# Output projection of a hybrid decoder step: from plain tiles to Strassen's scheme on halves, with tokens stationary

## The chip, the cores and the metric

The kernel runs on one NeuronCore of a Trainium2 chip. Five engines work side by side, each through its own instructions in order: TensorE (PE, with its weight loads shown apart as PEld), VectorE (DVE), ScalarE (ACT), GpSimd (POOL) and SyncE (SP), which here issues nearly all DMAs. The metric is the device time of one execution in microseconds; less is better. Matmul operands lie in SBUF (128 partitions), sums in PSUM (eight banks of 128 x 512 float32).

## The reference, cut to what matters

One layer of a hybrid decoder on 1024 prompt tokens with 16 meta tokens ahead of them, and on 32 sample tokens (8 sequences of 4) with 1024 cached positions each. The input projection feeds a stick-breaking attention group and a gated linear attention (GLA) group. Their gated outputs are joined and go through one output projection, a norm and a residual:

```python
mixed = jnp.concatenate([o_sb * jax.nn.silu(sg), o_gla * jax.nn.silu(gg)], axis=-1)
y = mixed @ w_out                      # 2048 features -> 2048 columns
x = x + rms_norm(y, norm_post_g)       # for 1024 prompt tokens and 32 sample tokens
```

All arithmetic is float32. A product of two float32 matrices is made on TensorE of three products: each operand is split into a high part (a cast to fp32r) and a low part (the remainder), and high x high, high x low and low x high are summed in PSUM.

## The kernel before, in words

The kernel is a row of stages, each one a scope of tile pools: transposing and normalising x, the attention heads with the input projection of their columns, GLA, the sample tokens' paged values, and the output projection. A small scheduler in the program, the `Weaver` (`W`), lays side work among the matmuls: a generator is put in with `W.spawn(gen, delay)`, and each `W.beat()` (one after each group of matmuls) runs the generators that are due; a generator's `yield n` asks for its next turn n beats later. Around this, the tile framework sets waits and the order of each engine's instructions: tiles of one tag share a fixed number of buffers, and a new tile waits until the tile whose buffer it takes has had its last reader. Work inside `urgent()` is ordered ahead of other work that is ready.

Weights of all projections come through `weight_chunk` (L174 to L183): a DMA of two blocks of 128 x 128 (128 KB, L177), a cast of the high part on ACT (L181), a subtraction for the low part on DVE (L182). The tags `wr`, `wh` and `wl` have three buffers each.

The gated mixture lies in DRAM as 16 tensors `md[k]`, features on partitions and 1056 token columns. The output projection (from L1158) takes the tokens in two halves `hf`: 512 prompt tokens and the 32 sample tokens together (544), then 512 prompt tokens. For each half `load_mix` (L1166) brings the sixteen `md` tiles into the SBUF slots `s0` to `s15` and splits them. Then for each of 16 blocks `c` of 128 output columns, eight weight chunks pass by, and `project` (L1264) does for each chunk and each column group 2 x 3 matmuls with the weights stationary and the tokens moving: two groups of 272 tokens in the first half, one of 512 in the second, and 256 for the last two blocks, whose split weights are kept in slots (`wk`) so that the last tokens can be finished in two parts. The result has output columns on partitions. `y_tok` (L1201) turns it with PE transposes through `yt` (L1274, L1207; samples L1216), squares it for the norm (L1210) and multiplies by the norm's gain into `y` (L1211). `finish0` (L1220) adds the residual for the first half in pieces of 256 columns (L1233, L1234, store L1236) while the second half is projected, and `finish1` (L1249) does it at the end for two tiles of 128 tokens at a time (L1253, `rstd_` L159 to L165, L1260, store L1262).

In the attention stage `z_feed` (L341 on) computes the sample tokens' scores from the cached keys `kp` on DVE (L376), one page per two beats, with loads on SP (L334).

## Time and profile before

| | |
|---|---|
| median of 3 runs | 2216.09 us (2214.83 to 2216.6) |
| profiled execution | 2214.65 us, its span 2212.9 us |
| busy share of the span | PE 97%, PEld 90%, DVE 72%, ACT 48%, POOL 4% |
| moved by DMA | 267.53 MB, 121 GB/s on average |
| first and last matmul of the output projection | start at 1801.4 and 2199.99 us |

The span runs from the first to the last instruction. A matmul's duration in a row contains its way through the array, and matmuls overlap; what a matmul costs on PE is the distance between the starts of two of them. A row of groups gives line, engine, operation, the output and inputs by the program's names, shapes, count, busy time, the mean of one in ns, and what ended the idle time before them. A row of the timeline begins with the start and the duration in microseconds. In a row of windows stand the stretch, the busy time of each engine with its instructions in brackets, the granted TensorE clock, the share of the sixteen DMA engines and GB/s.

### The profile page before, as it was taken

The page shows a single profiled execution, that of the slowest core. Times are in us where ns is not written, and L with a number is a line of the kernel's source. Part 1 is how long each engine was busy: PE and PEld are TensorE (multiplying, and loading weights), DVE is VectorE, ACT ScalarE, POOL GpSimd, SP SyncE. Part 2 cuts the span into 40 slices and gives each one's busy share as a digit, 9 for nine tenths or more (in the row PEclk, how much of TensorE's full clock was granted, in tenths as well). Part 3 has the DMA queues.
Part 4 walks back from the last instruction along what each step waited for, and adds up shares of the span by engine and source line. Part 5 has one row for each costly group of instructions (what it writes and reads, how often), then busy time and mean ns, then how long its engine had stood idle before and what let it go on. Part 6 is the DMA issues. An engine that isn't in the chain of part 4 may idle for free. (4 is left out here: it accounts for less than half of the span.)

```text
span 2212.9 us, 46718 instructions
## 1 busy us (share of the span) xinstructions
PE 2150.0 (97%) x13712; PEld 1988.2 (90%) x13712; DVE 1593.0 (72%) x6809; ACT 1059.4 (48%) x2900; POOL 87.2 (4%) x299
## 2 busy tenths in 40 slices
PE   6999999999999999999999999999999999999997
PEld 5999999999999989889998989987777899998786
DVE  7367777777777787887777888689999765335434
ACT  7355556555565555325243352444433355444443
POOL 0000010000100000200000000000000000000000
PEclk9999999999999999999999999999999999999999
DMA  6223343433433434324334343356666654225733
GB/s 190 63 75 104 83 106 94 102 105 80 108 97 95 105 80 126 108 74 106 102 89 114 83 116 82 90 161 194 201 193 193 191 179 142 86 84 170 238 96 134
DMA packets 411299, 267.53 MB, mean 121 GB/s; under 512 B 49378, under 2 KB 393890, under 8 KB 409890
## 3 DMA queue, kind: packets, MB, share of 16 engines
q1 hardware_dynamic: 408850, 264.27, 42.5%
q8 instruction: 108, 1.77, 0.3%
q14 instruction: 149, 1.22, 0.2%
q10 hardware_dynamic: 2192, 0.27, 0.1%
HBM read 223.47 MB, written 40.95 MB: 119 GB/s over the span
## 5 line engine op out<-in xcount | busy, mean ns | idle before, releaser
L376 DVE SCALAR_TENSOR_TENSOR jk<-kp,qb 128x128 f32<-128x128 f32 x2048 | 486.9, 287 | 40.9 <-DMA kp<-in_cache_k_dram 38.0
L286 PE MATMUL acc_g<-hT,wh_g 128*128 128x368 f32 (+2 forms) x768 | 258.0, 336 | 0.2
L287 PE MATMUL acc_g<-hT,wh_g 128*128 128x368 f32 (+2 forms) x768 | 247.6, 322 | 0.0
L288 PE MATMUL acc_g<-hT,wl_g 128*128 128x368 f32 (+2 forms) x768 | 246.9, 322 | 0.0
L1269 PE MATMUL oacc<-mx,wh_o 128*128 128x272 f32 (+1 forms) x736 | 238.8, 325 | 6.3 <-ACT wh_o L181 4.4
L1271 PE MATMUL oacc<-mx,wl_o 128*128 128x272 f32 (+1 forms) x736 | 235.5, 320 | 0.0
L1270 PE MATMUL oacc<-mx,wh_o 128*128 128x272 f32 (+1 forms) x736 | 234.8, 319 | 0.2 <-DVE mx L1186 0.2
L182 DVE TENSOR_TENSOR wl_o<-wr_o,wh_o 128x256 fp32r<-128x256 f32 x240 | 101.4, 425 | 152.4 <-ACT wh_o L181 146.3
L286 PEld LDWEIGHTS acc_g<-hT,wh_g 128*128 128x128 f32 x768 | 144.2, 188 | 33.6 <-issue 21.8
L376 DVE DVE_READ_ACCUMULATOR jk<-kp,qb 128x1 f32 x2048 | 166.0, 81 | 0.0
L181 ACT CAST wh_o<-wr_o 128x256 fp32r<-128x256 f32 x240 | 96.7, 405 | 138.7 <-PE oacc L1270 100.9
L1269 PEld LDWEIGHTS oacc<-mx,wh_o 128*128 128x128 f32 x736 | 139.1, 189 | 17.8 <-ACT wh_o L181 6.9
L1271 PEld LDWEIGHTS oacc<-mx,wl_o 128*128 128x128 f32 x736 | 138.6, 188 | 10.2 <-DVE wl_o L182 1.3
L1270 PEld LDWEIGHTS oacc<-mx,wh_o 128*128 128x128 f32 x736 | 138.9, 189 | 8.6 <-DVE mx L1186 0.5
L287 PEld LDWEIGHTS acc_g<-hT,wh_g 128*128 128x128 f32 x768 | 144.4, 188 | 1.1 <-issue 0.4
L288 PEld LDWEIGHTS acc_g<-hT,wl_g 128*128 128x128 f32 x768 | 144.3, 188 | 0.4 <-issue 0.4
L286 PE MATMUL acc_gv<-hT,wh_gv 128*128 128x384 f32 (+1 forms) x384 | 128.7, 335 | 0.0
L286 PE MATMUL acc_k<-hT,wh_k 128*128 128x378 f32 (+1 forms) x384 | 127.8, 333 | 0.0
L181 ACT CAST wh_g<-wr_g 128x256 fp32r<-128x256 f32 x128 | 51.7, 404 | 155.4 <-PE acc_g L287 140.1
L286 PE MATMUL acc_q<-hT,wh_q 128*128 128x368 f32 (+2 forms) x384 | 125.6, 327 | 0.0
L288 PE MATMUL acc_gv<-hT,wl_gv 128*128 128x384 f32 (+1 forms) x384 | 125.4, 327 | 0.0
L287 PE MATMUL acc_k<-hT,wh_k 128*128 128x378 f32 (+1 forms) x384 | 125.2, 326 | 0.0
(399 smaller groups left out, 5904.6 us busy)
## 6 DMA issues: line engine op xcount, KB each, us to landing
kp<-in_cache_k_dram SPq DMA_DIRECT2D x512, 64.0 KB
vr<-in_cache_v_dram SPq DMA_DIRECT2D x64, 512.0 KB
wr_o<-in_w_out_dram SPq DMA_DIRECT2D x256, 128.0 KB
qb<-qsd SPq DMA_DIRECT2D x64, 256.0 KB
wr_g<-in_w_in_dram SPq DMA_DIRECT2D x128, 128.0 KB
wr_v<-in_w_in_dram SPq DMA_DIRECT2D x64, 128.0 KB
wr_k<-in_w_in_dram SPq DMA_DIRECT2D x64, 128.0 KB
wr_q<-in_w_in_dram SPq DMA_DIRECT2D x64, 128.0 KB
```

The costliest lines, as they stand in the source:

```text
L181: act.copy(wh, raw[:])
L182: vec.tensor_tensor(wl, raw[:], wh.bitcast(F32), ALU.subtract)
L286: mm(acc[c][:, :n], wh[:, k2, :], hh[k][:, lo:hi], start=(k == 0), stop=False)
L287: mm(acc[c][:, :n], wh[:, k2, :], hl[k][:, lo:hi], start=False, stop=False)
L288: W.mark = mm(acc[c][:, :n], wl[:, k2, :], hh[k][:, lo:hi], start=False, stop=(k == NK - 1)).ins
L376: ins = vec.scalar_tensor_tensor(jk[:], kp[:], 1.0, qbs[h, b][:, t, :], ALU.mult, ALU.mult, accum_out=zt[:, t, NPG - 1 - i:NPG - i])
L1269: mm(o_, wh[:, k2, :], mh[:, lo:hi], start=(k == 0), stop=False)
L1270: mm(o_, wh[:, k2, :], ml[:, lo:hi], start=False, stop=False)
L1271: mm(o_, wl[:, k2, :], mh[:, lo:hi], start=False, stop=(k == NK - 1))
```

## The change

The output projection is written anew. Features, output columns and, within each half of 512 prompt tokens, tokens are cut in two: `A` (256 x 1024 blocks) times `W` (1024 x 1024 blocks). Seven products of half blocks take the place of eight (Strassen's scheme in Winograd's form). For each token half `hf` and each half `q` of the 1024 columns of a block, `run` goes through the seven products `p` in a written order; each product is four steps `i` of two feature tiles. The split token forms are stationary (128 tokens), 512 weight columns move, so the sums have tokens on partitions and no transposes are left. One step is 2 tiles x 2 token groups x 3 = 12 matmuls of 512 columns; in the products 1, 2, 7 and 3 of the first half 4 more for the 32 sample tokens, whose high and low parts stand side by side as one stationary operand of 64 columns. That is 4 x 7 x 4 x 12 = 1344 and 128 matmuls.

- `weight_forms` makes the four combined weight blocks during attention and GLA and writes them to DRAM (`td`): sixteen rounds with four loads of 256 KB, four subtractions of 128 x 512 on DVE and four stores of 256 KB, from beat 150 on, 40 beats apart.
- `weights` loads 512 KB per step, from `w_out` or `td`, into one of four `raw` buffers, and splits it into one of two places of a `ring` (in the slots `s2`, `s3`).
- `form_a11`, `form_a` and `form_s` load `md` into the same `raw` buffers, form the token combinations on DVE and split them into the slots. For the second half they run while the first half's last products are made, and at the start of its own.
- `into_y` adds each product's sums into tiles `y` of 128 x 512 (18 buffers), and where a tile is complete it squares it and multiplies it by the gain.
- `finish0` and `finish1` do norm and residual per 128 x 512 tile. At the very end the last product is done token group by token group, with its weights kept in slots, so that one tile of 128 tokens is left.

```diff
+    td = [dram.tile([P, 8, 1024], F32, name=f"td{j}") for j in range(4)]
...
+    def weight_forms():
+        for k in range(8):
+            for q in range(2):
+                t = dk.tile([P, 4, 512], F32, tag="tf", bufs=1, name=f"tf{k}_{q}")
+                for i, (r, c) in enumerate(((0, 0), (0, 1), (1, 1), (1, 0))):
+                    r0, c0 = 1024 * r + k * P, 1024 * c + q * 512
+                    nc.sync.dma_start(t[:, i, :], w_out[0, r0:r0 + P, c0:c0 + 512])
+                yield 12
+                vec.tensor_tensor(t[:, 0, :], t[:, 1, :], t[:, 0, :], ALU.subtract)
+                vec.tensor_tensor(t[:, 1, :], t[:, 1, :], t[:, 2, :], ALU.subtract)
+                yield 4
...
+                for j, i in enumerate((0, 2, 1, 3)):
+                    nc.sync.dma_start(td[j][:, k, q * 512:(q + 1) * 512], t[:, i, :])
+                yield 24
...
+        W.spawn(weight_forms(), 150, lasting=True)
...
+        def raw_tile(nm):
+            return op.tile([P, 1024], F32, tag="raw", bufs=4, name=nm)
+        def split(dst, src):
+            act.copy(dst[:, 0], src)
+            vec.tensor_tensor(dst[:, 1], src, dst[:, 0].bitcast(F32), ALU.subtract)
...
+        def form_a(hf):
+            for i in range(4):
+                keep(4 + i, pair(hf, 8 + 2 * i, f"rb{hf}_{i}"), 2 * i, f"fb{hf}_{i}", 2, 4)
+                yield 1
+        def form_s(hf):
+            for i in range(4):
+                u = pair(hf, 2 * i, f"ru{hf}_{i}")
+                v = pair(hf, 8 + 2 * i, f"rv{hf}_{i}")
...
+                vec.tensor_tensor(v1, u1, v1, ALU.add)
+                vec.tensor_tensor(u1, u1, u0, ALU.subtract)
+                vec.tensor_tensor(u0, v1, u0, ALU.subtract)
+                vec.tensor_tensor(v0, v0, u0, ALU.subtract)
+                yield 1
+                keep(8 + i, u, 2 * i, f"fu{hf}_{i}", 6, 7)
+                keep(12 + i, v, 2 * i, f"fv{hf}_{i}", 3, 5)
+                yield 1
...
+        def weights(p, q, i, nm, dst=None):
+            with urgent():
+                r = raw_tile(f"rw{nm}")[:].rearrange("p (k n) -> p k n", k=2)
...
+                nc.sync.dma_start(r, src)
+                if dst is None:
+                    j = next(turn) % 2
+                    dst = [t[:, j * 1024:(j + 1) * 1024].rearrange("p (k n) -> p k n", k=2) for t in ring]
+                act.copy(dst[0], r)
+                vec.tensor_tensor(dst[1], r, dst[0].bitcast(F32), ALU.subtract)
...
+        def product(bank, t, p, i, w, first, last):
+            for j in range(2):
+                a = forms[p, 2 * i + j]
+                ah, al = (a[:, s_, t * P:(t + 1) * P] for s_ in range(2))
+                mm(bank[t][:], ah, w[0][:, j], start=first and j == 0, stop=False, skip_group_check=True)
+                mm(bank[t][:], ah, w[1][:, j], start=False, stop=False, skip_group_check=True)
+                mm(bank[t][:], al, w[0][:, j], start=False, stop=last and j == 1, skip_group_check=True)
...
+        YB = 18
+        YO, XO, TO = (1, 4, 2, 6, 5, 7, 3), (6, 5, 7, 3, 1, 4, 2), (1, 6, 5, 2, 3, 7, 4)
+        run(0, 0, YO, dict(A="acc", B="B", D="D", E="D"), y[0], ssq[0], {})
+        run(0, 1, XO, dict(A="acc", B="B", D="D", E="B"), y[0], ssq[0],
+            {(3, 1): lambda: W.spawn(form_s(1), 2), (1, 1): lambda: W.spawn(form_a11(1), 1), (2, 1): lambda: W.spawn(form_a(1))})
+        W.spawn(finish0(y[0], ssq[0]))
+        W.spawn(finish_samples())
+        run(1, 0, YO, dict(A="acc", B="B", D="D", E="D"), y[1], ssq[1], {})
+        W.flush()
+        run(1, 1, TO, dict(A="acc", B="B", D="D", E="acc"), y[1], ssq[1],
+            {(1, 1): lambda: put_xr(0, 0), (3, 1): lambda: W.spawn(finish1(y[1], ssq[1], xr, (0, 1)), 1),
+             (7, 1): lambda: put_xr(2, 8), (4, 0): lambda: W.spawn(finish1(y[1], ssq[1], xr, (2,))),
+             (4, 1): lambda: W.spawn(finish1(y[1], ssq[1], xr, (3,)))})
-        def load_mix(hf):
-        def y_tok(hf, c, yt, y, ssq, tiles=(0, 1, 2, 3)):
-        def project(hf, kk, wh, wl, acc, yt, lo, hi):
...
-    nc = bacc.Bacc("TRN2", target_bir_lowering=False, num_devices=1)
+    nc = bacc.Bacc("TRN2", target_bir_lowering=False, num_devices=1, dynamic_dma_scratch_size=1024)
```

More of the change, by code (lines that the diff above doesn't have):

```diff
@@ new lines, in pair, with keep @@
+        def pair(hf, k, nm):
+            r = raw_tile(nm)[:].rearrange("p (k n) -> p k n", k=2)
+            for j in range(2):
+                nc.sync.dma_start(r[:, j, :], md[k + j][:, hf * 512:(hf + 1) * 512])
+            return r
+        def keep(i, r, k, nm, p0, p1):
+            f = slot(i, nm).rearrange("p (s k n) -> p s k n", s=2, k=2)
+            split(f, r)
+            for j in range(2):
+                forms[p0, k + j] = f[:, :, j, 0:256]
+                forms[p1, k + j] = f[:, :, j, 256:512]
@@ L1196, in hybrid_step @@
+        for _ in form_a11(0):
+            pass
+        ring += [slot(2 + i, f"ring{i}") for i in range(2)]
+        samples = sample_forms()
+        next(samples)
+        W.spawn(samples, 4)
+        W.spawn(form_a(0))
+        W.spawn(form_s(0), 4)
         gpost = op.tile([P, D], F32, tag="gpost", bufs=1, name="gpost")
         nc.sync.dma_start(gpost[:], norm_post_g[0].partition_broadcast(P))
-        ysm = op.tile([P, 4, P], F32, tag="ysm", bufs=1, name="ysm")
-        sssm = op.tile([P, 4], F32, tag="sssm", bufs=1, name="sssm")
@@ L1264, in project @@
-        def project(hf, kk, wh, wl, acc, yt, lo, hi):
-            o_ = acc[:, :hi - lo]
-            for k2 in range(2):
-                k = 2 * kk + k2
-                mh, ml = mix[hf, k]
-                mm(o_, wh[:, k2, :], mh[:, lo:hi], start=(k == 0), stop=False)
-                mm(o_, wh[:, k2, :], ml[:, lo:hi], start=False, stop=False)
-                mm(o_, wl[:, k2, :], mh[:, lo:hi], start=False, stop=(k == NK - 1))
-            if kk == NK // 2 - 1:
-                with urgent():
-                    act.copy(yt[:, lo:hi], o_)
-            W.beat()
```

297 lines of the change are left out of this document (172 added, 125 removed).

## The prediction

> **What bounds the kernel now.** I read the page's busy shares first, then the windows by stage.
>
> ```profile
> span 2212.9 us, 46718 instructions
> PE 2150.0 (97%) x13712; PEld 1988.2 (90%) x13712; DVE 1593.0 (72%) x6809; ACT 1059.4 (48%) x2900; POOL 87.2 (4%) x299
> ```
>
> ```profile
> 600.00:800.00 200.00, 198.35 (x1203) 184.50 (x1202) 154.73 (x806) 113.98 (x289) 17.71 (x58) 1.00 0.36 95
> 1900.00:2000.00 100.00, 100.00 (x805) 99.98 (x805) 38.52 (x103) 45.27 (x159) 0.00 (x0) 1.00 0.29 84
> 2000.00:2100.00 100.00, 97.05 (x472) 79.97 (x471) 50.75 (x143) 41.87 (x148) 0.00 (x0) 1.00 0.70 218
> 2030.00:2040.00 10.00, 10.00 (x47) 8.26 (x47) 4.65 (x13) 3.78 (x14) 0.00 (x0) 1.00 0.95 320
> 2200.30:2212.90 12.60, 0.44 (x2) 0.20 (x2) 6.63 (x14) 1.51 (x7) 0.00 (x0) 0.63 0.48 191
> ```
>
> PE is the bound in all stages; DVE, about half busy in the projection (1900 to 2100), has room there and less in attention (77% in 600 to 800). At 2030 the DMA engines are nearly full at 320 GB/s, or 337 at full share. After 2200.3 PE has no work left: that is the tail. So time falls only if PE's own work in the projection falls, or its waits or the tail. What PE pays per matmul is the distance of starts, in the timeline:
>
> ```profile
> 1925.10 0.29 PE L1269 MATMUL oacc<-mx,wh_o 128*128 128x272 f32 x1
> 1931.48 0.29 PE L1269 MATMUL oacc<-mx,wh_o 128*128 128x272 f32 x1
> 2149.79 0.39 PE L1269 MATMUL oacc<-mx,wh_o 128*128 128x512 f32 x1
> 2153.19 0.39 PE L1269 MATMUL oacc<-mx,wh_o 128*128 128x512 f32 x1
> 2153.65 0.39 PE L1271 MATMUL oacc<-mx,wl_o 128*128 128x512 f32 x1
> 2153.88 0.60 PE L1207 MATMUL yp<-ident,yt 128*128 128x128 f32 x4
> 2154.23 0.48 PE L1269 MATMUL oacc<-mx,wh_o 128*128 128x512 f32 x1
> ```
>
> Between the first two rows lie 51 matmuls of 272 columns: 6.38 / 51 = 0.1251 us each. Between the next two, 15 of 512: 3.40 / 15 = 0.2267. Four transposes cost 2154.23 - 2153.65 - 0.2267 = 0.35, or 0.088 each. A 256-column one, on the line through both matmul prices, is 0.1183 (an estimate).
>
> **PE's work, before and after.** Before: 1536 x 0.1251 = 192.2, 672 x 0.2267 = 152.3, 192 x 0.1183 = 22.7 and 144 transposes x 0.088 = 12.7, together 379.9 us. The stage runs from the first row below to the last, plus about 0.12 for the last matmul: 398.7. So it holds 18.8 us of waits.
>
> ```profile
> 1801.40 0.29 PE L1269 MATMUL oacc<-mx,wh_o 128*128 128x272 f32 x1
> 2199.99 0.28 PE L1271 MATMUL oacc<-mx,wk 128*128 128x256 f32 x1
> ```
>
> After: (1344 + 128) x 0.2267 = 333.7 us, 46.2 less. Of the eighth saved in the prompt's products, the 128 sample matmuls, which pay 512 columns each, take back 29.0. The Trainium skill (TensorE: Matmul & The Clock Gate, Back-to-back issue gap) gives a gap of N/2.4 + 2.5 ns, 215.8 ns for 512 and 115.8 for 272. By it PE's work would go from 356.6 to 317.7, 38.9 less, and the sum below would come out 7 us later; the trace has 226.7 ns, and I keep the rows.
>
> **The new waits.** The weights of a step are cast on ACT, then subtracted on DVE, now 1024 columns at a time into a ring of two places. The rows for such a chain:
>
> ```profile
> 2150.70 0.39 PE L1270 MATMUL oacc<-mx,wh_o 128*128 128x512 f32 x1
> 2151.12 0.41 ACT L181 CAST wh_o<-wr_o 128x256 fp32r<-128x256 f32 x1 [0.95 <-PE oacc L1270]
> 2151.57 0.42 DVE L182 TENSOR_TENSOR wl_o<-wr_o,wh_o 128x256 fp32r<-128x256 f32 x1 [0.93 <-ACT wh_o L181]
> ```
>
> ```profile
> L181 ACT CAST wh_o<-wr_o 128x256 fp32r<-128x256 f32 x240 | 96.7, 405 | 138.7 <-PE oacc L1270 100.9 <-DMA wr_o<-in_w_out_dram 32.0 <-PE oacc L1271 3.0
> L1185 ACT CAST mx<-mraw 128x544 fp32r<-128x544 f32 x16 | 9.9, 643 | 6.7 <-DMA mraw<-md 6.3 <-PE acc_g L288 0.4
> L1034 DVE TENSOR_TENSOR vvr<-vr 128x1024 f32<-128x1024 f32 x13 | 15.9, 1222 | 4.9 <-DMA vr<-in_cache_v_dram 4.0 <-PE dO L1043 0.9
> L1274 ACT COPY yt<-oacc 128x512 f32<-128x512 f32 x14 | 8.1, 582 | 3.7 <-PE oacc L1271 3.6
> L1234 DVE SCALAR_TENSOR_TENSOR y<-y,r_y,xr 128x256 f32<-128x256 f32 x32 | 14.3, 480 | 3.2 <-DMA xr<-in_x_prompt_dram 3.1
> L1260 DVE SCALAR_TENSOR_TENSOR y<-y,r_y,xr 128x512 f32<-128x512 f32 x8 | 5.5, 748 | 0.1
> ```
>
> ```profile
> L462 DVE TENSOR_TENSOR lo_s<-X,hi_s 127x512 fp32r<-127x512 f32 x43 | 29.6, 688 | 1.8 <-ACT hi_s L461 1.7
> ```
>
> The cast starts 0.42 after the start of the matmul that frees its buffer (0.19 after the array is free), the subtraction 0.04 after the cast's end. A cast of 1024 columns, on the line through 405 (256) and 643 ns (544), is 1.04 us; the subtraction 1.22. So a place freed at time 0 holds both parts at 0.19 + 1.04 + 0.04 + 1.22 + 0.06 = 2.55 us. PE meanwhile does one step, 12 x 0.2267 = 2.72, and needs the low part one matmul later, at 2.95. The chain has 0.40 us to spare, 1.3 in steps with samples (16 matmuls). DVE's whole work of the stage is 112 x 1.22 for weights, 28 x 1.22 + 32 x 0.69 for forms, 80 x 0.69 into y, 32 x 0.48 and 16 x 0.75 for the ends and some 8 for samples: 283 us, less than the stage. It is no bound, but an operation begun at the wrong moment makes a step late. The terms, each with its ends:
>
> (a) While forms are loaded they take every second raw buffer, so weights have two of the four. The cycle is then: subtraction done, DMA of 512 KB, cast, subtraction. The nearest 512 KB load:
>
> ```profile
> 1589.90 1.24 SPq L334 DMA_DIRECT2D vr<-in_cache_v_dram  x1
> 1594.57 1.23 DVE L1034 TENSOR_TENSOR vvr<-vr 128x1024 f32<-128x1024 f32 x1 [0.41 <-DMA vr<-in_cache_v_dram]
> ```
>
> 4.67 us, in a stretch with the DMA engines about two thirds busy. Then 4.67 + 1.04 + 0.04 + 1.22 + 0.1 = 7.07 for two steps, 3.53 each, against 2.72 or 3.63 with samples. Most form loads lie beside sample products; some 12 steps (product 4 twice, product 1 of the second half) do not: 12 x 0.81 = 10 us. Ends 0 and 18.
>
> (b) `finish0` and `form_a` of the second half lie on the first 16 steps of `run(1,0)`: 8.4 MB of weights, 8.4 of x and y, 2.1 of md, 18.9 MB in 43.5 us of PE. At 337 GB/s that is 56 us, 12.5 too many, of which the loads in hand cover some 4 (three steps, 8.2, less one load of 4.67); at 320, 59 us. I take 10, ends 0 and 15. That loads come late there already shows in the chain of waits, for loads a quarter as large:
>
> ```profile
> 2079.63 5.69 DMA wr_o<-in_w_out_dram
> ```
>
> The Trainium skill (DMA: Bandwidth & Descriptors, Specifications) puts the HBM limit per core at about 358 GB/s; by it these steps need 52.8 us and the term is 5 instead of 10. No row here goes over 337.
>
> (c) After the first product of `run(1,0)`, six new y tiles are due at 10.9 us and two of the 18 are free; the other four come with stores of `finish0`, whose norm starts some 5 us in. ACT waits there with the weight casts behind it: 3 us, ends 0 and 6. (d) The x tiles of the second half, 2 MB at once ahead of weights in SP's queue, 6.2 us of DMA at 337 GB/s against 8 us of weights in hand: 2, ends 0 and 4. (e) Evacuations: at the ends of 28 products adds on DVE (0.69) and copies on ACT (0.58) come in front of a cast or split. Both in front exceed the spare by 0.87; at 0.35 for each product 10 us, ends 0 and 28 x 1.27 = 36.
>
> The start costs nothing: the slots of the first forms and of the ring come free while the last gate's matmuls still run, as those of `mx` do now. Together 35 us of waits against 18.8. The stage becomes 368.7.
>
> **Tail.** Now one tile of 128 tokens is left, not two.
>
> ```profile
> 2200.30 0.37 ACT L1274 COPY yt<-oacc 128x256 f32<-128x256 f32 x1 [1.30 <-PE oacc L1271]
> 2202.53 0.18 DVE L1253 TENSOR_REDUCE tot<-yssq 128x2 f32<-128x32 f32 x1
> 2204.21 5.13 DVE L1260 SCALAR_TENSOR_TENSOR y<-y,r_y,xr 128x512 f32<-128x512 f32 x6
> ```
>
> 0.3 to the first evacuation, add 0.69, square 0.77, gain 0.69, reduction to residual 1.68 (2202.53 to 2204.21), four residuals 2.7, last store to the end 3.56 (2209.34 to 2212.9), and an estimated 1 for the tile before, still on DVE: 11.3, against 12.8 now.
>
> **Attention.** The tables cost 64 subtractions of 0.69, 44 us of DVE where 45 of each 200 us are free, 33.6 MB where DMA has a 0.36 share, and 128 issues on SP, at the row below 44 us of that queue. Idle time covers all three. But a store of `td` waits on SP for its subtraction with the next weight loads (L177) behind it, each round's 1 MB holds the rings 3.2 us, and a `kp` that comes late holds up DVE with the splits queued behind it:
>
> ```profile
> L334 SPq DMA_DIRECT2D kp<-in_cache_k_dram x431: 332/343/1421, 200.3 to 1327.2; - x144
> DVE jk L376 <- DMA kp<-in_cache_k_dram: 31.0, 21, 4.4
> ```
>
> The three weight buffers there cover about two chunks. I take 4 us, ends -2 (another order) and 40.
>
> **Sum.** 1801.4 + 4 + 368.7 + 11.3 = 2185.4 span; before it is 2212.9. The profiled execution is 1.75 above its span (2214.65) and the median 1.44 above that, so 2188.6: **2189**, 1.2% less. A change of 0.2%, some 4.4 us, is about what can be told from none.
>
> **Rivals.** *Bare gain* (0.17): waits stay at 18.8 and the tables are free: 2189 - 16 - 4 = 2169. For it, the largest of PE's direct waits in the stage, with its crowded DMA, is small; against it, three buffers became two.
>
> ```profile
> PE oacc L1269 <- ACT wh_o L181: 4.4, 5, 1.1
> ```
>
> *The ring decides, slower* (0.16): in half of the steps an add and a copy stand ahead of the cast and the split, 0.87 us each: 56 x 0.87 = 49 in place of (e): 2228. It ends over 2216 from a mean of (27 + 10) / 112 = 0.33 us per step on. For it: the spare of 0.40 is less than any one operation. Against it: weights are ordered first.
>
> *DMA decides* (0.08): weights 58.7, md 14.7, x and y 16.8, gain 1.0: 91.3 MB. If the stage gets only the 218 GB/s of 2000 to 2100, 419 us: 1801.4 + 4 + 419 + 11.3 + 3.2 = 2239. Against it: that window had idle DMA time, and 320 stands in the trace.
>
> *Tables on the path* (0.09): attention pays 38 and not 4: 2223. For it: DVE would be over 80% busy; against: PE lost only 1.65 us in 600 to 800.
>
> **How the numbers follow.** The forecast has 0.50, its own range 2172 to 2208. The range 2166 to 2232 holds it, the bare gain, the tables and half the ring; DMA and a ring in more than half the steps lie above. Faster: 0.50 + 0.17, less a little for its edge, 0.66; slower: ring, DMA and tables, less their near ends, 0.29; the same 0.05.
>
> **What would show it.** Starts 0.227 apart in 1472 matmuls, no L1207. Waits on the new split lines, in the second half's first run on weight DMAs; a stage of about 369 us that starts near 1805; 11 us after the last matmul. Wrong would be: waits of over 62 us in the stage, a DVE chain at 90% busy, or a start of the stage after 1820.

## The result and the profile after

| | before | after | forecast |
|---|---|---|---|
| median | 2215.5 us (4 runs) | 2268.2 us (4 runs, 2263.0 to 2269.1) | 2189 |
| profiled execution, its span | 2214.65, 2212.9 us | 2267.99, 2266.3 us | 2185.4 (span) |
| first matmul of the projection | 1801.4 | 1845.3 | 1805.4 |
| stage of the projection | 398.7 us | 408.6 us | 368.7 |
| PE's own work in it, waits in it | 379.9, 18.8 | 333.7, 74.9 | 333.7, 35 |
| after PE's last matmul | 12.8 | 12.5 | 11.3 |
| moved by DMA | 267.5 MB | 332.4 MB | - |

The ratio of after to before is 1.0233, with a 95% interval of 1.0215 to 1.0250: slower, on the other side of the forecast and above its range. The page of the changed kernel, its busy shares:

```profile
span 2266.3 us, 43753 instructions
PE 2129.8 (94%) x12640; PEld 1911.8 (84%) x12640; DVE 1712.3 (76%) x6719; ACT 1052.1 (46%) x2504; POOL 92.9 (4%) x299
```

Windows of the changed kernel (columns: window, its length, busy time and instructions of PE, PEld, DVE, ACT, POOL, then granted clock, DMA share, GB/s), and behind them two of the kernel before:

```profile
0.00:200.00 200.00, 163.02 (x935) 149.95 (x936) 119.15 (x376) 99.20 (x251) 6.83 (x29) 0.96 0.65 193
200.00:400.00 200.00, 187.00 (x1097) 174.56 (x1095) 158.44 (x776) 104.42 (x267) 22.12 (x54) 0.99 0.56 159
600.00:800.00 200.00, 199.99 (x1216) 191.62 (x1215) 156.24 (x812) 116.97 (x300) 18.93 (x65) 1.00 0.38 99
1900.00:2000.00 100.00, 97.52 (x414) 76.32 (x415) 58.17 (x68) 44.15 (x59) 0.00 (x0) 0.97 0.57 174
2000.00:2100.00 100.00, 76.41 (x295) 55.26 (x293) 71.62 (x102) 44.27 (x63) 0.00 (x0) 0.89 0.59 188
```

```profile
0.00:200.00 200.00, 178.63 (x1071) 166.87 (x1072) 117.71 (x444) 112.73 (x292) 10.96 (x45) 0.99 0.38 107
200.00:400.00 200.00, 200.00 (x1215) 192.19 (x1214) 154.45 (x812) 114.27 (x289) 16.77 (x56) 1.00 0.39 98
```

PE loses its time in two places: 28.6 us of busy time and 254 of 2286 matmuls in the first 400 us, where the DMA engines now move 193 and 159 GB/s instead of 107 and 98, and a quarter of the time from 2000 to 2100. In between, as from 600 to 800, nothing is lost. The first place is the tables' (rows: line, engine, operation, count; shortest, median and longest duration in ns; first and last start):

```profile
L394 SPq DMA_DIRECT2D tf<-in_w_out_dram x64: 327/424/1272, 42.8 to 355.8; - x64
L402 SPq DMA_DIRECT2D td<-tf x64: 319/327/779, 51.8 to 365.5; - x64
```

All sixteen rounds ran from 42.8 to 365.5 us. `yield 24` and the delay of 150 beats only set where these instructions stand in the order of the program; what the trace shows holding them back on the chip is the one buffer `tf` (SP waited 13.0 us before loads of `tf` for the stores of the round before, and 29.7 us before stores for the subtractions). VectorE, whose order is fixed, waited for the loads in its turn, and PE for splits that came late, in rows that the kernel before does not have (0 to 400 us; who waited, for whom: us in all, times, longest):

```profile
DVE tf L396 <- DMA tf<-in_w_out_dram: 19.4, 7, 5.4
PE z L516 <- ACT hi_s L480: 8.0, 5, 5.3
```

Now the second place. The timeline of PE gives where each product begins, for instance

```profile
1845.27 0.39 PE L1397 MATMUL A<-ring,fa 128*128 128x512 f32 x1
1874.50 0.40 PE L1397 MATMUL E<-ring,fb 128*128 128x512 f32 x1
2030.87 0.73 PE L1397 MATMUL E<-ring,fb 128*128 128x512 f32 x2 [0.70 <-ACT ring L1285]
2058.91 0.73 PE L1397 MATMUL A<-ring,fb 128*128 128x512 f32 x2 [1.37 <-ACT ring L1285]
2188.51 0.39 PE L1397 MATMUL B<-ring,fu 128*128 128x512 f32 x1
2199.39 0.39 PE L1397 MATMUL D<-ring,fv 128*128 128x512 f32 x1
2253.60 0.39 PE L1399 MATMUL E<-wk,fb 128*128 128x512 f32 x1
```

An undisturbed product takes 2199.39 - 2188.51 = 10.88 us, which is 48 x 0.2267, and 14.51 with 16 sample matmuls. Against that, each product's distance to the next gives its loss (us, from 28 such starts; the framework mixes some neighbouring products, so a product is counted as its number of matmuls in PE's order):

| run, products in order | loss of each | sum |
|---|---|---|
| `run(0,0)`: 1, 4, 2, then 6, 5, 7, 3 | 14.7, 3.4, 8.9, then 0.3 together | 27.3 |
| `run(0,1)`: 6, 5, 7, 3, then 1, 4, 2 | 1.1 together, then 1.2, 17.2, 3.7 | 23.2 |
| `run(1,0)`: 1, 4 and 2, then 6, 5, 7, 3 | 10.8, 8.5, then 5.0 together | 24.4 |
| `run(1,1)`: all seven | 0 | 0 |

Together 74.9 us. The losses lie where forms are loaded or where the first half is finished, and nowhere else. PE's waits in the stage, 1840 to 2254 us (line waited for, in all, times, longest):

```profile
PE E L1397 <- ACT ring L1285: 18.8, 5, 8.6
PE sc L1432 <- DVE sf_a L1199: 12.6, 1, 12.6
PE A L1397 <- ACT ring L1285: 8.2, 5, 4.8
PE D L1398 <- DVE ring L1286: 2.6, 2, 1.6
```

The weights' high part (ACT) is late, for up to 8.6 us at a time; the low part, on which the ring's spare of 0.40 us hung, is late by 1.6 us at most. One wait of 12.6 us is that of the sample forms. SP's queue in that first product, and in the second half's first product:

```profile
1856.25 2.45 SPq L1255 DMA_DIRECT2D sm<-md  x5
1859.10 0.32 SPq L421 DMA_DIRECT2D md<-gs  x1
1859.47 5.20 SPq L1255 DMA_DIRECT2D sm<-md  x11
...
2079.30 0.38 SPq L1281 DMA_DIRECT2D rw<-in_w_out_dram  x1
2079.74 1.88 SPq L1355 DMA_DIRECT2D xr<-in_x_prompt_dram  x4
2081.66 4.90 SPq L1373 DMA_DIRECT2D xs<-in_x_sample_dram  x8
2086.66 2.85 SPq L1355 DMA_DIRECT2D xr<-in_x_prompt_dram  x2
2089.59 1.09 SPq L1357 DMA_DIRECT2D out_dram<-y  x2
2090.78 0.46 SPq L1218 DMA_DIRECT2D rb<-md  x1
2091.33 1.52 SPq L1281 DMA_DIRECT2D rw<-td  x3
```

The sample loads `sm` stand between the last gate groups' stores `md<-gs` (L421), since both use the stage buffers; the last of them is out only at 1864.7. Later eight small loads `xs`, six `xr` and two stores stand ahead of the weights `rw`, 16 issues, and one load of a form: 12 us from one weight load to the next.

### The profile page after: what moved, and what is told of

Same layout as the page of the kernel before. It is cut to its first block, busy times and chain, and to the rows that moved or that the text cites. A ratio compares the mean times of both kernels' runs of the same rounds, so it can differ in the third digit from the quotient of the medians.

```text
span 2266.3 us, 43753 instructions
## 1 busy us (share of the span) xinstructions
PE 2129.8 (94%) x12640; PEld 1911.8 (84%) x12640; DVE 1712.3 (76%) x6719; ACT 1052.1 (46%) x2504; POOL 92.9 (4%) x299
## 3 DMA queue, kind: packets, MB, share of 16 engines
q1 hardware_dynamic: 392082, 329.28, 50.2%
## 4 chain that ended last, share of the span: by engine, by line
PE 38%; DVE 8%; DMA 6%; ACT 2%; issue 2%; SPq 0%; DVEq 0%; ACTq 0%
PE acc_g L287 4%; PE acc_g L288 3%; PE acc_g L289 3%; PE acc_gv L287 3%; PE acc_gv L289 3%; PE acc_gv L288 3%; DVE ring L1286 1%; PE dO L1063 1%; PE P L777 1%; DMA Sb<-in_state_gla_dram 1%; PE D L1398 1%; PE D L1399 1%; PE D L1397 1%; PE B L1398 1%; PE B L1397 1%
## 5 line engine op out<-in xcount | busy, mean ns | idle before, releaser
L1286 DVE TENSOR_TENSOR ring<-rw,ring 128x1024 fp32r<-128x1024 f32 x108 | 132.1, 1223 | 105.9 <-ACT ring L1285 105.4
L1285 ACT CAST ring<-rw 128x1024 fp32r<-128x1024 f32 x108 | 113.3, 1049 | 168.8 <-PE sc L1432 42.6
L287 PE MATMUL acc_gv<-hT,wh_gv 128*128 128x384 f32 (+1 forms) x384 | 129.1, 336 | 0.0
L287 PE MATMUL acc_q<-hT,wh_q 128*128 128x368 f32 (+2 forms) x384 | 126.0, 328 | 1.1 <-ACT kraw L600 1.1
L288 PE MATMUL acc_gv<-hT,wh_gv 128*128 128x384 f32 (+1 forms) x384 | 125.6, 327 | 0.0
L289 PE MATMUL acc_k<-hT,wl_k 128*128 128x378 f32 (+1 forms) x384 | 125.2, 326 | 0.0
L289 PE MATMUL acc_q<-hT,wl_q 128*128 128x368 f32 (+2 forms) x384 | 123.6, 322 | 0.0
L288 PE MATMUL acc_q<-hT,wh_q 128*128 128x368 f32 (+2 forms) x384 | 123.3, 321 | 0.0
L502 ACT ACTIVATE X<-X 127x512 f32<-127x512 f32 (+4 forms) x112 | 55.0, 491 | 141.3 <-DVE X L501 141.1
L287 PE MATMUL acc_v<-hT,wh_v 128*128 128x378 f32 x336 | 115.1, 343 | 5.1 <-DVE q L611 5.1
```

The source lines that it names most:

```text
L287: mm(acc[c][:, :n], wh[:, k2, :], hh[k][:, lo:hi], start=(k == 0), stop=False)
L288: mm(acc[c][:, :n], wh[:, k2, :], hl[k][:, lo:hi], start=False, stop=False)
L289: W.mark = mm(acc[c][:, :n], wl[:, k2, :], hh[k][:, lo:hi], start=False, stop=(k == NK - 1)).ins
L502: act.activation(X, X, AF.Exp)
L1285: act.copy(dst[0], r)
L1286: vec.tensor_tensor(dst[1], r, dst[0].bitcast(F32), ALU.subtract)
```

## Experiments on the tables

A time from one run is given without an interval. The changed kernel's four runs lie 6 us apart, and fifteen runs of the kernel before, taken later, 11 us (2208.6 to 2219.9), so that some 8 us between two single runs mean nothing. "Start" is the first matmul of the projection; by it the first 1800 us are read apart from the stage. It too differs from profile to profile: from 1841.9 to 1845.3 in the six profiles of the changed kernel's attention code (this one and e3, e4, e5, e8 and e10 below), so that 3 us of start mean nothing either.

**Hold the loads to their beats.**

```diff
-                    nc.sync.dma_start(t[:, i, :], w_out[0, r0:r0 + P, c0:c0 + 512])
+                    d = nc.sync.dma_start(t[:, i, :], w_out[0, r0:r0 + P, c0:c0 + 512])
+                    tc.add_manual_dep(d.ins, W.mark.name, NOSYNC, reason="spread")
```

> The changed kernel with one edit: each load of the weight tables is ordered behind the matmul that was last when its beat came, so that the sixteen rounds keep their 40 beats of distance. The work is the same. Theory A (the tables cost because the planner ran all of them between 43 and 366 us, at 160 to 240 GB/s, in front of the weight loads): the projection's first matmul comes back from 1845.3 to 1800 to 1808, the total to 2224 to 2232. Rival B (the 44 us are the price of the tables' 33.6 MB and 64 subtractions wherever they stand): the projection still starts at 1835 or later, total 2255 or more.

Measured: 2254.2 us, ratio 1.0175 (1.0156 to 1.0195). The loads now start from 254.8 to 1054.2 us, and the projection at 1832.3. That lies between the two theories and nearer to B: being crowded costs 13 us, and 31 of the 44 us of delay remain when the same work is spread over 800 us.

**Leave the tables out.**

```diff
-        W.spawn(weight_forms(), 150, lasting=True)
...
```

> Leaves out the weight tables: products 4 to 7 read plain blocks of the output weights with the same transfer shapes, so their results are not the products of the combined weights. Theory A: the tables are the whole of the later start, so the projection begins at 1801 to 1804 and the total is 2222 to 2227; the projection keeps its 408 us. If part of the later start has another cause (a pool or queue that the change moved), it begins at 1815 or later.

Measured: 2230.3 us, start 1804.9; the stage takes 411 us instead of 409. So the tables are 40 of the 44 us, and the other 3.5 are about what the start differs between profiles of one code.

**Only the DMAs of the tables; the subtractions on GpSimd.** Both on top of the paced loads. The first leaves the four subtractions of each round out, the second does this with all four:

```diff
-                vec.tensor_tensor(t[:, 0, :], t[:, 1, :], t[:, 0, :], ALU.subtract)
+                nc.gpsimd.tensor_tensor(t[:, 0, :], t[:, 1, :], t[:, 0, :], ALU.subtract)
```

> The paced tables of e1_tables_paced, with the loads and the stores but without the 64 subtractions: the tables then hold plain quarters of the weights, so the output projection's sums are left wrong. Theory A (VectorE's 44 us and its waits are the cost): projection from 1804-1812 us, time 2224-2234 us. Rival B (traffic and issues): start over 1826, time over 2248 us. Start between 1812 and 1826: both have a share, read from how far it lies from 1804.9 and from 1832.3.

> The paced tables of e1_tables_paced (2254.2 us, projection from 1832.3), with their 64 subtractions moved from VectorE to GpSimd. Theory A (what the tables cost is their 64 x 0.69 = 44 us of VectorE and its waits for their loads, in an engine that works through attention in a fixed order): the projection starts at 1804-1815 us, time 2225-2237 us. Rival B (the cost is the 33.6 MB of traffic and its 128 issues on SP): start over 1826, time over 2248 us. If GpSimd's own masks then wait behind the subtractions, the attention's GpSimd waits rise and the time lies between or above.

Measured: with the DMAs alone 2247.2 us, start 1825.8. Of the 27.4 us between 1804.9 and 1832.3 the subtractions, with their waits for loads, are 6.5, the loads and stores 20.9, each give or take the 3 us by which starts differ. On GpSimd the subtractions make it 2294.9 us, start 1873.5. The rows of VectorE's wait for page loads (200 to 1000 us) in the kernel without tables and in the one with the DMAs alone, then GpSimd's subtractions in e6:

```profile
DVE jk L377 <- DMA kp<-in_cache_k_dram: 28.4, 18, 3.8
```

```profile
DVE jk L377 <- DMA kp<-in_cache_k_dram: 48.8, 34, 5.3
```

```profile
L397 POOL TENSOR_TENSOR tf<-tf x16: 1263/1300/1940, 262.0 to 1092.2; 128x512 f32<-128x512 f32 x16
```

A subtraction takes 1300 ns there where VectorE's median is 692; the Trainium skill (GPSIMD Engine Reference, Elementwise — side-by-side cycle accounting) has a ratio of 1.96 for a two-input addition, and this is 1.88. GpSimd also stood before loads of `tf` with the attention's masks (L508, L524) queued behind it; ScalarE's waits for the mask L524 rose from 9.0 us in e1 to 23.0. That is 14 us of waits against a start 41 us later; the rest was not traced. An idle engine that has a place in the chain is no free engine. By e7, theory B (traffic and issues) holds for some three quarters of the cost, theory A for one quarter.

**Cut the bursts; deepen the page buffers.** Again on top of the paced loads. The first gives each load and each store of the tables a beat of its own, the second more page buffers (and `while fetched < n + 5` in `z_feed`), the third the same buffers without tables.

```diff
                 for i, (r, c) in enumerate(((0, 0), (0, 1), (1, 1), (1, 0))):
                     r0, c0 = 1024 * r + k * P, 1024 * c + q * 512
...
+                    paced(t[:, i, :], w_out[0, r0:r0 + P, c0:c0 + 512])
+                    yield 4
...
```

```diff
-            kps[h, b, i] = dk.tile([P, P], F32, tag="kp", bufs=3, name=f"kp{b}_{h}_{i}")
+            kps[h, b, i] = dk.tile([P, P], F32, tag="kp", bufs=5, name=f"kp{b}_{h}_{i}")
```

> e1_tables_paced sent its 64 loads of 256 KB in bursts of four (1 MB) and its stores likewise; here each load and store is held to a beat of its own (one load every 4 beats, one store every 2), and the subtractions come one every 2 beats; work and total beats a tile as before. Theory A (a burst of 1 MB stands in front of the page loads kp, for which VectorE waited 48.8 us with the tables' DMA alone against 28.4 us without): VectorE's waits for kp from 200 to 1000 us fall to 35 us or less, the projection starts at 1815-1824 us instead of 1832.3, time 2237-2246 us. Rival B (the 33.6 MB cost what they cost, however they are cut): start at 1829 or later, time over 2250 us.

> e1_tables_paced with five page buffers kp instead of three, so that the page loads are issued five pages ahead. Theory A (with the tables' transfers a page load that lands later than two pages of VectorE's work, some 5 us, makes VectorE wait): the waits for kp fall below 15 us (30.7 in e1), and the start of the projection to 1810-1822 us, time 2232-2244. Rival B (VectorE's order, not the page loads, carries the tables' cost): start over 1828, time over 2248.

> The changed kernel without its tables (as e2_no_tables: the weights of products 4 to 7 are plain quarters, so the projection's sums are left wrong), with five page buffers instead of three. Theory A (five buffers help only because the tables' transfers delay page loads): projection from 1801-1806 us, time 2226-2232, as e2 (1804.9, 2230.3). Rival B (page loads cost something without the tables too, and five buffers would speed the kernel before as well): start below 1799 us, time below 2224.

Measured: cut finer, the page waits fall from 30.7 to 17.0 us and the start is later all the same, 1837.8 (2257.9 us): a miss, and theory B. Five page buffers take the waits to 5.2 us, start 1822.9 (2244.2 us), just outside what theory A expected. But without tables five buffers bring the start from 1804.9 to 1797.5 as well (2220.9 us), so that some 7 of the 9 us are not the tables' at all (rival B): page loads cost something without them too. With five buffers and paced loads the tables still cost 1822.9 - 1797.5 = 25.4 us. What carries these (bandwidth, the place of 128 more issues on SP, or VectorE's fixed order) the runs don't tell apart. One reading fits them all: VectorE's waits for any load, from 200 to 1000 us, are 28.4 us without tables, 52.8 in e1, 50.2 with the DMAs alone and 53.4 cut finer, where 36.4 are for the tables' own loads instead of 19.4; with five page buffers they are 3.0 without tables and 24.3 with them. Each time the tables add 21 to 25 us of such waits, and the start is 21 to 33 us later; less waiting for pages did not help where waiting for `tf` took its place. That VectorE's order carries the cost is argued from this, not shown. Spreading helps further: see the last part of the next section.

## Experiments on the stage

**Sample loads early.** The samples' features go into idle buffers `wr` and are asked for before the gate's last stores; the second half of them four beats later.

```diff
-            sm = [stage(f"sm{i}")[:, :256].rearrange("p (k n) -> p k n", n=NSMP) for i in range(2)]
+            sm = [wp.tile([P, 2, P], F32, tag="wr", name=f"sm{i}")[:].rearrange("p a (b n) -> p (a b) n", n=NSMP) for i in range(2)]
...
```

> The changed kernel with one edit: the sample columns of md are loaded into buffers of their own (the small weight buffers that stand free), and only the eight tiles that the first sample operand needs are loaded at the start, the other eight four beats later. Theory A (PE's 12.6 us wait in the first product is for loads that stood behind the last gate group's work): that wait falls to under 3 us, the first product from 29.2 to 15 to 19 us, the total to 2253 to 2260. Rival B (the wait only moves, since the form loads are late too): the first three products together keep their 66.9 us within 4.

Measured: 2252.7 us. The first product takes 15.7 us instead of 29.2, the first three together 52.9 instead of 66.9. Theory A. The stage is 14.5 us shorter.

**Finishing loads and stores on GpSimd's queue.**

```diff
-                        nc.sync.dma_start(x, x_prompt[0, i * P:(i + 1) * P, b * 512 + f * 256:b * 512 + (f + 1) * 256])
+                        nc.gpsimd.dma_start(x, x_prompt[0, i * P:(i + 1) * P, b * 512 + f * 256:b * 512 + (f + 1) * 256])
...
-                    nc.sync.dma_start(y_prompt[0, i * P:(i + 1) * P, b * 512:(b + 1) * 512], y[i, b][:])
+                    nc.gpsimd.dma_start(y_prompt[0, i * P:(i + 1) * P, b * 512:(b + 1) * 512], y[i, b][:])
...
```

> The changed kernel with one edit: the loads of x and the stores of y of the first token half (finish0 and the samples' x) are issued from GpSimd's queue, not SP's. The bytes are the same. Theory A (in the second half's first run, weight loads stand on SP behind loads and stores that wait for the norm): the first product there falls from 21.7 to 11 to 14 us, the next two from 30.3 to 22 to 26, total 2247 to 2256. Rival B (DMA bandwidth, the term I had priced): the two stay within 4 us of 52.0 together, total 2262 or more.

Measured: 2257.3 us. Product 1 of `run(1,0)` falls from 21.7 to 12.9 us, 4 and 2 stay (31.6), 6 grows by 5.9 and 5, 7 and 3 come back to 10.88. So SP's order was 8.8 us of the first product, as the rows of SP above have it; behind it stands something else, and `run(1,0)` as a whole gains 6.6 us. The Trainium skill (DMA: Bandwidth & Descriptors, Issuing engines are not separate DMA queues) says that another issuing engine saves only the time to start a DMA, mostly small. Here it saved waiting in line: 16 issues, two of them held up for 2.0 and 1.4 us, ahead of a weight load.

**Raw buffers of their own.** The forms' tiles take a tag `fraw` with two buffers, the weights keep `raw` with three.

```diff
-        def raw_tile(nm):
-            return op.tile([P, 1024], F32, tag="raw", bufs=4, name=nm)
+        def raw_tile(nm, tag="raw", bufs=3):
+            return op.tile([P, 1024], F32, tag=tag, bufs=bufs, name=nm)
...
-        YB = 18
+        YB = 16
```

> Alone changed: the weights of the projection get three raw buffers of their own and the token forms two of theirs (before: four shared), and the y tiles go from 18 buffers to 16 to make room. Theory A (a weight load stands behind the buffer that a form's split has to free): the waits of the products that run beside forms - fourth and third product of run(0,0) 3.4 and 8.9 us, the last two of run(0,1) 17.2 and 3.7, the first three of run(1,0) 19.3, together 52 us - fall under 30 us, and the time from 2268.2 to 2240-2253 us. Rival B (VectorE's and ScalarE's work on the forms, or the DMA bandwidth, makes these waits, whoever owns the buffers): they stay over 42 us, and the time at 2260 or more. If 16 y tiles are too few, run(1,0) and run(1,1) show new waits of evictions on y stores.

Measured: 2241.5 us, the largest step of all; the stage is 24.0 us shorter. In `run(0,0)` products 4 and 2 lose 2.1 us instead of 12.3, in `run(0,1)` products 1, 4 and 2 lose 0.3 instead of 22.1. The rows of the changed kernel show how a form held up the weights (DVE's split of a form, then SP's load of weights into the buffer it freed, then ACT, waiting):

```profile
2041.07 1.22 DVE L1199 TENSOR_TENSOR fa<-ra,fa 128x1024 fp32r<-128x1024 f32 x1
...
2042.31 0.37 SPq L1281 DMA_DIRECT2D rw<-td  x1
...
2046.47 1.04 ACT L1198 CAST fu<-ru 128x1024 fp32r<-128x1024 f32 x1 [8.67 <-DVE ru L1242]
2047.42 1.04 ACT L1285 CAST ring<-rw 128x1024 fp32r<-128x1024 f32 x1
```

The load goes out 0.02 us after the form's split ends at 2042.29, and the cast of those weights stands behind a form's cast that waited 8.67 us for its own data. VectorE was the crowded engine there (4.91 of 5 us busy from 2035 to 2040), and yet the loss went with the buffers. Since four shared buffers became three and two, the run does not tell the separation from the fifth buffer. In `run(1,0)` products 4 and 2 lose 24 us now instead of 8.5, and product 1 loses 4.1 instead of 10.8: part of the gain is handed back there. The 16 y tiles are not the reason: ScalarE's waits there for stores of y are 4.7 us, against 5.4 with 18. PE now waits 13.8 us for casts of the form `fb`, and those 8.0 us for its loads, which go out on SP among the finishing steps' loads and stores.

**The three together, then another order.** e8 joins the last three edits; e10 adds to it the order of `run(1,0)`, asks for the x tiles two steps ahead and lets the forms `fb` of the second half come one in two beats.

```diff
-        run(1, 0, YO, dict(A="acc", B="B", D="D", E="D"), y[1], ssq[1], {})
+        run(1, 0, XO, dict(A="acc", B="B", D="D", E="B"), y[1], ssq[1], {})
```

> The three edits of the projection stage together: sample loads early in other buffers (e4: -15.6 us), the finishing loads and stores on GpSimd's queue (e5: -10.9 us), raw buffers split with 16 y tiles (e3). The tables are as in the changed kernel. Theory A (these are three separate waits): the gains add up, and the stage falls from 408.5 us to 409 - 26.5 - gain of e3, about 360-368 us if e3 gives 15 to 22. Rival B (behind each wait stands another late thing, VectorE's forms or the weights' bandwidth, so that what one edit gives the next takes): the stage stays over 375 us.

> e8_stage_three (2228.7 us; run(1,0) lost 27 us there, its second and third product 20) with two more edits: run(1,0) takes the products in the order 6, 5, 7, 3, 1, 4, 2, so that it needs two new y tiles a product instead of six after the first, and so that the forms fa and fb of the second half may come later (one in 2 beats); and the x tiles of the finishing steps are asked for two steps ahead. Theory A (in run(1,0) VectorE stands in its fixed order before an x tile that was asked for just then, and the y tiles are wanted too early): the losses of run(1,0) fall from 27 to under 12 us, time 2206-2214 us. Rival B (run(1,0) is at the limit of the DMA engines, 0.82-0.94 busy from 2040 to 2110 in e8): the same bytes still have to pass, the losses move to later products and stay over 20 us, time over 2221 us.

Measured: 2228.7 us with the three. In the stage the single gains, 14.5 + 8.2 + 24.0 = 46.7, come to 36, since e3 and e5 both end in `run(1,0)`, which lost 27 us there; the stage is 372.6 us, where three separate waits would have made it 362. With the other order 2228.0 us: `run(1,0)` loses 24, now spread over its products 6, 5, 7, 3 and 1. Rival B's numbers (over 20 us, over 2221) came true for this step. Windows of e10:

```profile
2060.00:2070.00 10.00, 6.26 (x20) 4.71 (x19) 7.51 (x15) 3.84 (x5) 6.71 (x13) 0.77 0.95 321
...
2080.00:2090.00 10.00, 7.79 (x33) 5.64 (x31) 6.04 (x11) 3.17 (x4) 5.23 (x10) 1.00 0.93 286
2090.00:2100.00 10.00, 6.07 (x24) 4.35 (x24) 6.13 (x11) 3.14 (x3) 5.13 (x11) 0.97 0.92 311
```

With the queue and the buffers out of the way the DMA engines are 0.92 to 0.95 busy at 286 to 321 GB/s in the windows from 2060 to 2100, where PE loses most. In the changed kernel itself the window where `run(1,0)` lost most shows about two thirds of that rate, and the engines full only behind it:

```profile
2087.00:2097.00 10.00, 3.15 (x15) 2.29 (x13) 5.39 (x20) 2.65 (x6) 0.00 (x0) 0.92 0.69 202
2127.00:2137.00 10.00, 10.00 (x45) 8.26 (x44) 7.74 (x10) 4.96 (x8) 0.00 (x0) 1.00 0.98 306
```

There the queue decided, as e5 shows. That bandwidth was next in line is argued from these shares: in the last row full engines cost PE nothing.

**All together, tables slower, finishing held.** e12_all takes every edit that helped, with e10's order, and lets the finishing steps run on into `run(1,1)`, whose order becomes 6, 5, 1, 2, 3, 7, 4; the second spreads the tables from beat 100 with 56 beats a round; e14 also holds the finishing steps to their beats.

```diff
-                    yield 1
+                    yield 1 if n < 12 else 3
```

```diff
-        W.spawn(weight_forms(), 150, lasting=True)
+        W.spawn(weight_forms(), 100, lasting=True)
```

```diff
-                vec.scalar_tensor_tensor(y[i, b][:, fs], y[i, b][:, fs], r[:, i:i + 1], xs.pop(n), ALU.mult, ALU.add)
+                ins = vec.scalar_tensor_tensor(y[i, b][:, fs], y[i, b][:, fs], r[:, i:i + 1], xs.pop(n), ALU.mult, ALU.add)
+                tc.add_manual_dep(ins.ins, W.mark.name, NOSYNC, reason="spread")
...
-                mm(bank[t][:], al, w[0][:, j], start=False, stop=last and j == 1, skip_group_check=True)
+                W.mark = mm(bank[t][:], al, w[0][:, j], start=False, stop=last and j == 1, skip_group_check=True).ins
```

> All the edits that helped, together: tables paced, five page buffers kp, sample loads early, raw buffers split with 16 y tiles, finishing loads and stores on GpSimd's queue and asked for ahead, run(1,0) in the order 6, 5, 7, 3, 1, 4, 2, and, new, the finishing steps after the first six y tiles only every third beat, on into run(1,1), whose order becomes 6, 5, 1, 2, 3, 7, 4 so that it wants y tiles later. Theory A (the causes found are separate, and run(1,0)'s 24 us of loss in e10 are its 0.89-0.95 busy DMA engines, which spreading relieves): projection from 1820-1824 us as in e9_tables_kp5, stage 368-378 us, time 2202-2214 with the loss of run(1,0) unchanged, 2188-2201 with it halved or better, in any case faster than before (2214). Rival B (run(1,0) is late for another reason, its weight loads behind SP's order): loss stays over 20 us, time over 2205.

> e12_all with the tables spread over more of the attention: from beat 100 instead of 150, 56 beats a tile instead of 40. Theory A (the rest of the tables' cost, 17.8 us of start in e9_tables_kp5, comes from how densely their 33.6 MB lie among the page loads): start at 1806-1816 us and 6 to 14 us faster than e12_all. Rival B (each byte and each subtraction costs about the same wherever it lies): start within 4 us of e12_all's and the time too.

> e12_all_slow_tables (2203.8 us) spread the finishing steps by beats alone, and they ran all the same from 2033.3 to 2077.0 us, 44 us, where their beats cover nine products, some 100 us. Here each of them is also held to the last matmul before its beat (a dependence that only orders, without a semaphore, as the page scores have). Theory A (run(1,0)'s loss, 21.1 us in e12_all_slow_tables, is the finishing steps' 8.4 MB packed into the 50 us in which the DMA engines are 0.9-0.99 busy): the finishing steps then last 80 us or more, the DMA share there falls below 0.85, the loss to 12 us or less, the time to 2192-2198. Rival B (the loss is not the finishing steps' traffic, but the second half's forms and the turn of the banks): loss stays over 18 us, time 2200 or more.

Measured: 2208.9 us for e12_all (10 runs), ratio to before 0.9974 (0.9963 to 0.9985): the gain is there, 0.3%. `run(1,0)` still loses 20.0 us in it and `run(1,1)` 5.5, 25.5 together where e10 has 25.9, so that spreading by beats relieved nothing. With the slower tables 2203.8 us, 0.9944 (0.9925 to 0.9963), start 1819.0 instead of 1825.5: density costs 5 to 7 us, less than theory A's 6 to 14 and more than rival B's 4. Held finishing steps: 2200.3 us, 0.9939 (0.9921 to 0.9956). The rows of the finishing steps in e12_all_slow_tables and in e14:

```profile
L1368 DVE SCALAR_TENSOR_TENSOR y<-y,r_y,xr x32: 476/481/489, 2033.3 to 2077.0; 128x256 f32<-128x256 f32 x32
```

```profile
L1368 DVE SCALAR_TENSOR_TENSOR y<-y,r_y,xr x32: 472/478/485, 2031.0 to 2118.7; 128x256 f32<-128x256 f32 x32
```

Beats alone had let them run in 44 us, as they did the tables; held, they take 88. Yet `run(1,0)` still loses 17.1 us (21.1 before), 16 of them in its first four products, and the two medians' runs overlap. So traffic may be part of that loss; theory A's 12 us did not come true, and the loss is a little under rival B's 18. The largest single piece is neither theory's, a copy into a new y tile that waited for a store and held up PE (1990 to 2190 us):

```profile
PE B L1411 <- ACT y L1340: 3.8, 1, 3.8
ACT y L1340 <- DMA out_dram<-y: 9.2, 3, 5.2
```

The rest stays open. e14 is the fastest kernel here, 15 us under the kernel before. The five page buffers are part of that, by the 7 us of e13, and they have nothing to do with the change; the kernel before was not run with them.

## Why the prediction was wrong

The forecast had PE's saving of 46.2 us right and missed what surrounds it. By its own terms:

- **PE's work, 333.7 us: right.** Starts are 0.2267 apart in undisturbed products (10.88 us for 48).
- **Attention, 4 us with ends -2 and 40: measured 44, of which 40 are the tables.** This is the step that turned the sign. "Idle time covers all three" was the failed sentence. Each resource had idle time on average; late loads that hold up an engine in its fixed order, which the text named, were priced at a tenth of the 40 us; the page loads that it had in mind are only one kind of them, for with five page buffers and 5.2 us of waits for pages the tables still cost 25 us. Two things were missed. The forecast took "from beat 150 on, 40 beats apart" for times, where `z_feed` beside it (the order-only dependence at L379 of the kernel before, against `W.mark`) shows that a beat by itself holds nothing on the chip; and even paced, 33.6 MB and 128 issues cost 21 us (e7) in spite of 22% idle time on VectorE. The tables' rival had this, at 38 us and a chance of 0.09.
- **Start of the stage, 0: measured 14.7.** The forecast looked at the slots and the ring, and left out `sample_forms`, whose buffers are the gate's. Moving its loads took the 14.7 to 1.2 (e4).
- **(a) Shared raw buffers, 10 with ends 0 and 18: measured 34.4** (products 4, 2 and 1, 4, 2 beside forms), of which e3 took 31.9. The cycle was taken as a weight load that always has two buffers. In truth a load waits until the form ahead of it is added, cast and split, with that form's own load and ACT's queue in it: 8.67 us in one place, not 0.81 a step. e3, which gives the forms buffers of their own and one more in all, is the run behind this.
- **(b), (c) `run(1,0)`, 13 together: measured 24.4.** Right place; but 8.8 us of the first product were, by e5, SP's order (16 issues ahead of a weight load), not bandwidth. With the queue free e10 loses 24 us there too, at DMA shares of 0.92 to 0.95, and e14, with the finishing steps spread, 17: what of that is bandwidth stays open. The ceiling of 337 GB/s was low (e12_all_slow_tables moved 353 from 2060 to 2070, at a share of 0.99). Term (c) is seen, as 5.4 us of ScalarE's waits for stores of y, and in e14 as 3.8 us of PE's.
- **(d) x tiles, 2: none. (e) Evacuations, 10 with ends 0 and 36: 1.4** in the 15 products that run beside neither forms nor finishing. The ring of two places with its 0.40 us of spare was no risk there; the rival that hung on it (0.16) had the wrong cause.
- **Tail, 11.3 (its terms add up to 11.4): 12.5.**

Sum: 1845.3 + 333.7 + 74.9 + 12.5 = 2266.4, against a span of 2266.3. Two of the three signs named beforehand as showing it wrong came true, waits over 62 us and a start after 1820; the third, a DVE chain at 90% busy, only for some microseconds beside forms (0.72 from 2000 to 2100). The rivals with the right place, tables and DMA, were added to the range one at a time; they came together.

## What to carry to other kernels

Side work is free only if something on the chip holds it where it was put and if the engines it uses have slack in their order, not in their average: look at what a program's pacing becomes (first and last start of each group) before counting idle time. When two streams share buffers or a queue, the urgent one runs at the pace of the other one's slowest chain, so price the whole chain to the release (load, add, cast, split), not the urgent stream's own cycle. A saving in the bound engine's work must be followed through the places where its feeders have other duties: here 46 us saved met 56 us of new waits in the stage and 44 ahead of it, and the version that pays (0.6%, with an edit that is not the change's among its parts) came only after each of these places had been worked on.

## What the runs showed of the hardware

After some of the waits TensorE's matmuls come at half speed for some microseconds. In the changed kernel's timeline, around a wait that ended at 2077:

```profile
2077.09 0.50 PE L1397 MATMUL A<-ring,fa 128*128 128x512 f32 x1 [2.69 <-ACT A L1333]
2077.67 0.39 PE L1399 MATMUL A<-ring,fa 128*128 128x512 f32 x1
2077.89 0.40 PE L1397 MATMUL A<-ring,fa 128*128 128x512 f32 x1
...
2080.12 0.63 PE L1399 MATMUL A<-ring,fa 128*128 128x512 f32 x1
2080.54 0.63 PE L1397 MATMUL A<-ring,fa 128*128 128x512 f32 x1
2080.97 0.63 PE L1398 MATMUL A<-ring,fa 128*128 128x512 f32 x1
...
2082.01 0.39 PE L1399 MATMUL A<-ring,fa 128*128 128x512 f32 x1
2082.24 0.40 PE L1397 MATMUL A<-ring,fa 128*128 128x512 f32 x1
```

They lie 0.22 to 0.23 us apart at first, 0.42 to 0.43 a little later, and 0.23 again from 2082 on. The granted clock in the windows around it:

```profile
2074.88:2078.29 3.41, 1.20 (x5) 1.02 (x6) 1.79 (x3) 2.90 (x5) 0.00 (x0) 1.00 0.39 146
2078.29:2081.70 3.41, 3.41 (x9) 2.67 (x9) 3.29 (x7) 1.22 (x3) 0.00 (x0) 0.50 0.61 165
```

The clock was halved for 3.41 us, after 3.41 us in which PE was busy 35% of the time (1.20 us). In this trace the clock changes only after whole steps of 3.41 us (the seven half-clock stretches of the stage last one to four). Counted in such steps from 60 to 2240 us, PE was busy 49% or less in the step before each of the 13 falls of the clock, and 48% or more in each step after which the clock stayed full; so the limit lies near half a step of work here. In the stage 46 matmuls stand 0.42 to 0.43 apart, in seven places: 46 x 0.20 = 9.2 us of the 74.9 are not waiting but the clock after it. The prediction had no term for that. The Trainium skill (TensorE: Matmul & The Clock Gate, HAM oscillation) has the clock halved by gaps of over some 3.4 us, and N/1.2 ns for a matmul then (Back-to-back issue gap), 427 for 512 columns. The trace agrees on the pace; of the gap, this place shows it after a wait of 2.7 us.
